# Weights stand and tokens move in 26 chunks of a decoder block on one Trainium2 core

## Chip, core and metric

The kernel runs on one NeuronCore of one Trainium2 chip. The metric is device time in microseconds for one execution. The profile shows one execution of the same program with every instruction of TensorE (PE, with its weight loads as PEld), VectorE (DVE), ScalarE (ACT), GpSimd (POOL) and the DMA queue of SyncE (SP).

## What is computed

One decoder layer on 256 tokens of width 2048, in float32: a SwiGLU feed-forward block, a token mixer (sparse attention beside multi-scale retention), and a second feed-forward block, each behind a modulated RMS norm. Cut to what the change touches:

```
h = modulate(x, ...)                              # 256 x 2048
x = x + 0.5*gt1 * (silu(h @ w_gate) * (h @ w_up)) @ w_down      # d_ff = 5632, once before and once after the mixer
u = modulate(x, ...)
q, kv, gate_logits, q_r, k_r, v_r, g_r, ga, gb = split(u @ w_in)
k_cmp, v_cmp = compress(kv[:, 0]), compress(kv[:, 1])           # 15 blocks of 32 tokens, stride 16, per group
    # compress: gelu((block + pos) @ cmp_w1 + b1) @ cmp_w2      # cmp_w1: 32*128 x 128
retention: scores = (q_r @ k_r.T) * decay ...
gates = sigmoid(gate_logits)
```

## The kernel before

**Parts.** A float32 operand is split in two parts that TensorE takes at full rate: `hi`, the operand rounded to fp32r by ScalarE, and `lo`, the remainder, by VectorE (`split`). A product is hi·hi + hi·lo + lo·hi. Activations have parts `ahi` and `alo` (tiles of 128 x 4 x 256, the model dimension on partitions), weights `whi` and `wlo`.

**Units and chunks.** All weights pass through one stream. A unit is 512 KB of it: one raw tile of 128 x 1024 (`raw`, six buffers), split to `whi` and `wlo` (four buffers each, lines 136 and 137). `run` issues loads as raw tiles come free and splits up to four items ahead of the unit that TensorE works on. A `chunk` computes 256 tokens x 512 outputs with the contraction over 16 tiles of 128: eight units, each 2 contraction tiles x 512 columns. In `unit`, tokens stand (128 x 128 of `ahi` or `alo` is the loaded operand) and weights move, 512 columns at a time: three matmuls for each half of the tokens and each contraction tile (lines 239 to 241), 96 in a chunk. The moving operand is read by turns: element j, then element j + 256, which lies 1 KB away (`by_turns`); `halves` undoes that when the result is read.

**What follows a chunk.** The result has tokens on partitions. Where it is next a contraction operand it is turned by eight TensorE transposes of 128 x 128 (`to_banks`, line 480): the gate·up product of every feed-forward chunk (`transposed`), the retention queries and keys (`retention.tr`), and the two compressed projections (`compress.tr`). Such later steps are put on a list, and one step is taken after each unit (`push`, `soon`).

**Around it.** `compress` multiplies 32 slices of the first layer in plain float32, 60 columns moving (line 923); its weights `cmp_w1` are loaded ahead, into free activation tiles (line 858). `gate_logits` takes 48 matmuls of 256 columns (lines 969 to 971). The first feed-forward block overlaps its first 6 chunk pairs with the modulation vectors (`early`, lines 688 to 690); loads for modulation (`w_ada`) are spread over the stream all along.

Of the kernel before, what the change touches and what calls it, by code (L numbers as in the profile page):

```python
# [18 lines left out]
P = 128  # L19
# [49 lines left out]
def block_kernel(ctx: ExitStack, tc: tile.TileContext, I, konst, decay, out):  # L69
# [9 lines left out]

    def act_hi(dt=F32R):  # L80
        return ap_.tile([P, 4, S], dt, tag="ahi", name="ahi")

    def act_lo(dt=F32R):
        return ap_.tile([P, 4, S], dt, tag="alo", name="alo")
# [550 lines left out]
    def ffn(l, his, los, last, first=None, head=None):  # L635
# [24 lines left out]

        def transposed(c, g):
# [61 lines left out]
        def both(c):  # L723
            g = [] if first and 2 * c < EARLY else chunk(act, src(wg, c), KT, NCH, gate_done(c), head=None if c else head)
# [127 lines left out]
    w1 = [[], []]  # L852
    for i in range(2):
        def ld(i=i):
            for b in range(4):
                w = act_hi(F32) if i == 0 else act_lo(F32)
                w = w.rearrange("p a s -> p (a s)").rearrange("p (j e) -> p j e", e=DH)
                nc.sync.dma_start(w, I["cmp_w1"][0, i, b * 8 * P:(b + 1) * 8 * P, :].rearrange("(j p) e -> p j e", p=P))
                w1[i].append(w)
        if i == 0:  # L860
            items.insert(len(items) - 60, ("do", lambda: clear()))
        at = len(items) - 10 - 8 * i
        items.insert(at, ("do", ld))
# [9 lines left out]
    def seg_chunk(c0, width, s, g, n, done):  # L873
# [4 lines left out]
        return chunk(u, src, KT, s * n, done)  # L878
# [17 lines left out]

    def compress(i):
        def done(ps):
            z = evac(ps)
            box = {}  # L900

            def tr():
                zT = t4([P, 4, S])
                banks = to_banks(lambda t, k: z[:, t, k * P:(k + 1) * P])
                for b in range(2):
                    nc.vector.tensor_copy(zT[:, 2 * b:2 * b + 2], banks[b])
                zp = []
                for h in range(2):
                    zz = t4([P, GROUPS, NCMP, 16])
                    src = bass.AP(tensor=zT.tensor, offset=zT.offset + 16 * h,  # L910
                                  ap=[list(zT.ap[0]), [S, GROUPS], [16, NCMP], [1, 16]])
                    pb = pos[:, i, 16 * h:16 * h + 16][:, None, None, :].to_broadcast([P, GROUPS, NCMP, 16])
                    nc.vector.tensor_tensor(zz, src, pb, op=ALU.add)
                    zp.append(zz)
                box["zp"] = zp

            def first_layer(b):
                def f():
                    if b == 0:
                        box["ps"] = mx()  # L920
                    for jj in range(8):
                        j = 8 * b + jj
                        nc.tensor.matmul(box["ps"][:, :60], w1[i][b][:, jj, :],  # L923
                                         box["zp"][j // 16][:, :, :, j % 16], start=j == 0, stop=j == 31)
                    if b == 3:
                        g = small(60, "g60")
                        nc.scalar.activation(g, box["ps"][:, :60], AF.Gelu_apprx_tanh, bias=b1[:, i:i + 1])
                        box["g"] = g
                return f

            def second_layer():
                g = box["g"]
                ps2 = mx()
                if i == 1:
                    for k in range(GROUPS):
                        nc.tensor.matmul(ps2[0:NCMP, k * DH:(k + 1) * DH], g[:, k * NCMP:(k + 1) * NCMP],
                                         w2[:, 1, :], start=True, stop=True)
                    v = ps2[0:NCMP, :].rearrange("p (g d) -> p g d", g=GROUPS)
                    for r in (0, 64):
                        nc.scalar.activation(vc[r:r + NCMP], v, AF.Copy)  # L940
                    nc.vector.tensor_tensor(vc[32:32 + NCMP], v, vc[0:NCMP].bitcast(F32), op=ALU.subtract)
                    return
                nc.tensor.matmul(ps2[0:60, :DH], g, w2[:, 0, :], start=True, stop=True)
                kn = t2([P, DH])
                junk = t2([P, DH])
                sc = small(1, "s1")
                nc.vector.tensor_copy(kn[0:60], ps2[0:60, :DH])
                nc.vector.scalar_tensor_tensor(junk[0:60], kn[0:60], 1.0, kn[0:60], op0=ALU.mult, op1=ALU.mult,
                                               accum_out=sc[0:60])
                nc.gpsimd.tensor_scalar(sc[0:60], sc[0:60], 1.0 / DH, EPS, op0=ALU.mult, op1=ALU.add)  # L950
# [9 lines left out]
            if i == 0:  # L960
                push(None, to_kcT)
# [415 lines left out]
```

## Time and profile before

| | us |
|---|---|
| median of three runs (2462.95 to 2465.0) | 2462.95 |
| the profiled execution | 2464.18 |
| its span, first to last instruction | 2462.4 |
| PE busy | 2425.2 |
| DVE busy | 1738.0 |
| ACT busy | 1219.8 |

PE is busy for 98% of the span and carries 88% of the chain that ended last. In the last feed-forward block (from 1800 us) the DMA engines move about 200 GB/s at 0.6 of their time, and DVE is busy for about half.

### The profile page before, as it was taken

How to read it: one execution, taken by the hardware profiler on the slowest of the kernel's cores; microseconds unless marked ns; L12 is line 12 of the kernel's file. 1: busy time of each engine (PE TensorE's matmuls, PEld its weight loads, DVE VectorE, ACT ScalarE, POOL GpSimd, SP SyncE). 2: the span in 40 equal slices, each digit the busy share in tenths (PEclk: the TensorE clock that was granted, in tenths of full speed). 3: DMA queues.
4: the chain of work that ended last, by engine and by line, in shares of the span. 5: the costliest groups of instructions: out<-in, count | busy, mean ns of one | idle time of the engine just before them, and what ended most of it. 6: DMA issues, size and time to landing. Idle time of an engine off the chain costs nothing.

```text
span 2462.4 us, 31664 instructions
## 1 busy us (share of the span) xinstructions
PE 2425.2 (98%) x11616; PEld 2116.0 (86%) x11616; DVE 1738.0 (71%) x2044; ACT 1219.8 (50%) x1584; POOL 139.8 (6%) x134
## 2 busy tenths in 40 slices
PE   6999999999999999999999999999999999999999
PEld 4888888888888888888888888888888888888887
DVE  7778878989656478886667777777788554555555
ACT  4788644444445455564444444444644444444443
POOL 1000001010010111200000000000000010001001
PEclk9999999999999999999999999999999999999999
DMA  9999888899776555667887777886599666666664
GB/s 354 337 323 344 286 318 310 294 314 341 273 231 193 148 150 171 193 215 268 281 269 257 250 256 256 274 269 235 180 342 325 203 205 198 197 202 202 202 199 152
DMA packets 348264, 616.65 MB, mean 250 GB/s; under 512 B 22096, under 2 KB 79926, under 8 KB 347852
## 3 DMA queue, kind: packets, MB, share of 16 engines
q1 hardware_dynamic: 347852, 614.51, 74.5%
q8 instruction: 91, 1.49, 0.2%
q14 instruction: 65, 0.53, 0.1%
q0 software_dynamic: 256, 0.12, 0.0%
HBM read 612.45 MB, written 2.10 MB: 250 GB/s over the span
## 4 chain that ended last, share of the span: by engine, by line
PE 88%; DVE 6%; DMA 3%; issue 2%; ACT 1%; POOL 0%; SPq 0%; DVEq 0%; ACTq 0%
PE accb L240 24%; PE accb L241 24%; PE accb L239 24%; PE accb L690 3%; PE accb L688 3%; PE accb L689 3%; DVE wlo L137 2%; DVE aacc L372 2%; DMA raw<-in_w_ffn_down_dram 2%; PE mx L480 1%; DMA raw<-in_w_ada_dram 1%; PE mx L923 1%; PE mx L1160 1%; ACT whi L136 1%; PE mx L1108 0%
## 5 line engine op out<-in xcount | busy, mean ns | idle before, releaser
L137 DVE TENSOR_TENSOR wlo<-raw,whi 128x1024 fp32r<-128x1024 f32 x852 | 1048.6, 1240 | 581.9 <-ACT whi L136 576.2
L136 ACT ACTIVATE whi<-raw 128x1024 fp32r<-128x1024 f32 x852 | 893.3, 1056 | 892.8 <-PE accb L241 690.8
L239 PE MATMUL accb<-whi,ahi 128*128 128x512 f32 x3072 | 1175.3, 383 | 1.3 <-ACT ahi L537 0.9
L240 PE MATMUL accb<-wlo,ahi 128*128 128x512 f32 x3072 | 1166.1, 380 | 3.4 <-DVE wlo L137 2.5
L241 PE MATMUL accb<-whi,alo 128*128 128x512 f32 x3072 | 1165.2, 379 | 1.2 <-DVE alo L605 1.2
L240 PEld LDWEIGHTS accb<-wlo,ahi 128*128 128x128 f32 x3072 | 580.8, 189 | 88.9 <-DVE wlo L137 5.6
L241 PEld LDWEIGHTS accb<-whi,alo 128*128 128x128 f32 x3072 | 580.6, 189 | 85.7 <-DVE alo L556 1.7
L239 PEld LDWEIGHTS accb<-whi,ahi 128*128 128x128 f32 x3072 | 580.8, 189 | 82.4 <-ACT ahi L537 2.0
L372 DVE SCALAR_TENSOR_TENSOR aacc<-raw,cond,aacc 128x1024 f32<-128x1024 f32 x270 | 352.0, 1304 | 1.7 <-DMA raw<-in_w_ada_dram 0.7
L626 POOL TENSOR_TENSOR x<-x,t 128x512 f32<-128x512 f32 x50 | 80.9, 1641 | 1553.0 <-DVE t L621 1553.0
L688 PE MATMUL accb<-whi,ahi 128*128 128x512 f32 x384 | 146.6, 382 | 0.0
L690 PE MATMUL accb<-whi,alo 128*128 128x512 f32 x384 | 145.8, 380 | 0.4 <-DVE alo L802 0.4
L689 PE MATMUL accb<-wlo,ahi 128*128 128x512 f32 x384 | 146.0, 380 | 0.0
L690 PEld LDWEIGHTS accb<-whi,alo 128*128 128x128 f32 x384 | 72.7, 189 | 11.1 <-DVE alo L802 0.8
L689 PEld LDWEIGHTS accb<-wlo,ahi 128*128 128x128 f32 x384 | 72.7, 189 | 10.6 <-DVE wlo L137 0.5
L688 PEld LDWEIGHTS accb<-whi,ahi 128*128 128x128 f32 x384 | 72.9, 190 | 10.1
L605 DVE TENSOR_TENSOR alo<-mx,ahi 128x512 fp32r<-128x512 f32 x52 | 33.5, 686 | 29.4 <-ACT ahi L604 29.3
L604 ACT ACTIVATE ahi<-mx 128x512 fp32r<-128x512 f32 x52 | 28.3, 597 | 46.9 <-PE mx L480 46.9
L621 DVE TENSOR_TENSOR t<-accb,gt 128x512 f32<-128x512 f32 x56 | 36.2, 684 | 7.8 <-PE accb L241 7.8
L647 ACT ACTIVATE t<-accb 128x512 f32<-128x512 f32 x44 | 25.7, 596 | 28.6 <-PE accb L241 20.3
L1123 ACT ACTIVATE t<-t,m 128x256 f32<-128x256 f32 (+1 forms) x64 | 28.2, 443 | 18.5 <-DVE m L1114 18.5
L883 ACT ACTIVATE t<-accb 128x512 f32<-128x512 f32 x44 | 25.8, 596 | 22.8 <-PE accb L241 22.7
(196 smaller groups left out, 1049.9 us busy)
## 6 DMA issues: line engine op xcount, KB each, us to landing
raw<-in_w_ada_dram SPq DMA_DIRECT2D x288, 512.0 KB, 5.7
raw<-in_w_ffn_gate_dram SPq DMA_DIRECT2D x176, 512.0 KB, 5.1
raw<-in_w_ffn_up_dram SPq DMA_DIRECT2D x176, 512.0 KB, 4.7
raw<-in_w_ffn_down_dram SPq DMA_DIRECT2D x176, 512.0 KB, 4.2
raw<-in_w_in_dram SPq DMA_DIRECT2D x176, 512.0 KB, 4.5
raw<-in_w_in_dram SPq DMA_DIRECT2D x128, 256.0 KB, 3.9
raw<-in_w_proj_nsa_dram SPq DMA_DIRECT2D x32, 512.0 KB, 5.8
raw<-in_w_proj_ret_dram SPq DMA_DIRECT2D x32, 512.0 KB, 5.6
```

Source lines behind the costliest of these rows:

```text
L136: nc.scalar.activation(hi_ap, raw_ap, AF.Copy)
L137: nc.vector.tensor_tensor(lo_ap, raw_ap, hi_ap.bitcast(F32), op=ALU.subtract)
L239: nc.tensor.matmul(ps[t], xh, wh, start=kt == 0, stop=False)
L240: nc.tensor.matmul(ps[t], xh, wl, start=False, stop=False)
L241: nc.tensor.matmul(ps[t], xl, wh, start=False, stop=kt == K - 1)
L372: nc.vector.scalar_tensor_tensor(box[0], raw, k, box[0], op0=ALU.mult, op1=ALU.add)
L605: nc.vector.tensor_tensor(lo[:, 2 * b:2 * b + 2], ps, h.bitcast(F32), op=ALU.subtract)
L621: nc.vector.tensor_tensor(in_two(y), halves(ps[t]), in_two(gt[:, n * NCH:(n + 1) * NCH]), op=ALU.mult)
L626: engine.tensor_tensor(xs, xs, y, op=ALU.add)
L688: nc.tensor.matmul(ps[t], xh, wh, start=kt + a == 0, stop=False, **kw)
L689: nc.tensor.matmul(ps[t], xh, wl, start=False, stop=False, **kw)
L690: nc.tensor.matmul(ps[t], xl, wh, start=False, stop=kt + a == k0 + nk - 1, **kw)
```

## The change

`turned_chunk` is new. It computes the same 256 tokens x 512 outputs as two sub-chunks of 256 outputs; a unit is now 4 contraction tiles x 256 columns. The weights stand, 128 x 128 at a time, and the tokens move: one matmul of `whi` against both token parts (512 columns, into the two halves of a bank) and one of `wlo` against the hi part (256 columns, added to the first half). `parts_by_turns` reads the tokens: element j, then element j + 128, which lies 512 bytes away. The result has outputs on partitions, so it is not transposed; `added` adds the two halves of the bank with a `tensor_reduce` on VectorE and puts the tokens in order. For that the two parts of an activation lie in one tile (`act_pair`).

It is used for the gate and up chunks 1 to 10 of the second feed-forward block (chunk 0 stays), retention's queries and keys (4 chunks) and the two compressed projections: 26 chunks of 512 outputs. Beside it:

- `cmp_w1` comes through the weight stream in eight loads and is split; a first-layer step multiplies parts of the blocks (120 columns stand) with 256 moving columns, and `fold` adds the parts afterwards in one small matmul. 
- The gate logits take 16 matmuls of 512 columns, both weight parts standing (96 columns).
- The mixer now begins with the keys and values of attention group 0, which take the `head` of the norm; the two compressed projections follow, then the gate logits and the queries of group 0.
- Retention's scores stand two units earlier on the list, since no transposes lie between.

```diff
+    def parts_by_turns(his, los, kt):
+        h, l = his[kt // 4][:, kt % 4], los[kt // 4][:, kt % 4]
+        return bass.AP(tensor=h.tensor, offset=h.offset,
+                       ap=[list(h.ap[0]), [l.offset - h.offset, 2], [1, P], [P, 2]])
+
+    def turned_chunk(his, los, src, K, done):
+        ps = []
+        def step(c, kt):
+            def f(hi, lo):
+                if kt == 0:
+                    ps[:] = [mx([P, 2, S]) for _ in range(2)]
+                for b in range(2):
+                    for a in range(4):
+                        k, bs = kt + a, slice(b * P, (b + 1) * P)
+                        both = parts_by_turns(his, los, k)
+                        nc.tensor.matmul(ps[b], hi[:, a, bs], both, start=k == 0, stop=False, skip_group_check=True)
+                        nc.tensor.matmul(ps[b][:, 0], lo[:, a, bs], both[:, 0], start=False, stop=k == K - 1,
+                                         skip_group_check=True)
+                if kt + 4 == K:
+                    done(c, ps)
+            return f
+        return [("w", src(kt, 4, c), 4, 256, step(c, kt)) for c in range(2) for kt in range(0, K, 4)]
+
+    def added(o, ps):
+        for b in range(2):
+            nc.vector.tensor_reduce(o[:, b].rearrange("p (t j) -> p j t", t=2),
+                                    ps[b].rearrange("p h (j t) -> p j t h", t=2), axis=AX.X, op=ALU.add)
...
+        def gate_turned(c):
+            def f(i, ps):
+                if i == 0:
+                    sg[c] = t4((P, 4, S))
+                g = sg[c][:, 2 * i:2 * i + 2]
+                added(g, ps)
+                nc.scalar.activation(g, g, AF.Silu)
+            return f
+        def up_turned(c):
+            def f(i, ps):
+                y = t2([P, 2, S])
+                added(y, ps)
+                g = sg[c][:, 2 * i:2 * i + 2]
+                nc.vector.tensor_tensor(g, y, g, op=ALU.mult)
+                if i == 1:
+                    push(*[None] * GAPS[0], in_parts_of(c, sg.pop(c)))
+            return f
...
-                        nc.tensor.matmul(box["ps"][:, :60], w1[i][b][:, jj, :],
-                                         box["zp"][j // 16][:, :, :, j % 16], start=j == 0, stop=j == 31)
...
+                    nc.tensor.matmul(box["ps"][0:120], box["Z", j // 16][:, j % 16].rearrange("p a c -> p (a c)"),
+                                     W[:, :, jj].rearrange("p a e -> p e a"), start=j == 0, stop=j == 31)
...
+            nc.tensor.matmul(ps[0:96], gl[kt // 8][:, kt % 8].rearrange("p a c -> p (a c)"), parts_by_turns(u_hi, u_lo, kt),
+                             start=kt == 0, stop=kt == KT - 1)
...
+    kv, q = attention(0)
+    mix += kv + z_chunk(0, done0) + after_units(z_chunk(1, done1), quarters0, 4)
+    mix += [("a", rows(win, 0, KT, O_GL, 48), KT, 48, gate_raw), ("do", gate_logits)]
+    mix += after_units(q, quarters1, 4)
...
-            push(None, tr, None, scores(0), scores(1))
+        def qk_done(c, ps):
+            if c == 0:
+                box["qkT"] = t4([P, 4, S])
+            added(box["qkT"][:, 2 * c:2 * c + 2], ps)
+            if c == 1:
+                dec = t2([P, 2, S])
+                nc.sync.dma_start(dec, decay[:, 2 * qd:2 * qd + 2, :])
+                box["dec"] = dec
+                push(None, scores(0), scores(1))
```

Three places of the program, as the instructions stand on an engine. On TensorE in the last feed-forward block before, `accb` is a chunk's bank, `t4` the gate·up product, `kc` the identity; the transposes stand two units into the next chunk:

```order
L239 MATMUL accb_15936<-whi_15903,ahi_14776 128x512
L240 MATMUL accb_15936<-wlo_15904,ahi_14776 128x512
L241 MATMUL accb_15936<-whi_15903,alo_14777 128x512
L480 MATMUL mx_15969<-kc_75,t4_15754 128x128 x4
L480 MATMUL mx_15974<-kc_75,t4_15754 128x128 x4
L239 MATMUL accb_15935<-whi_15923,ahi_14862 128x512
L240 MATMUL accb_15935<-wlo_15924,ahi_14862 128x512
```

And on TensorE now, at the seam of two sub-chunks of that block (`mx` is a sub-chunk's bank, `act` a tile with both token parts):

```order
L318 MATMUL mx_15737<-act_15057,whi_15762 128x512
L319 MATMUL mx_15737<-act_15057,wlo_15763 128x256
L318 MATMUL mx_15852<-act_14867,whi_15787 128x512
L319 MATMUL mx_15852<-act_14867,wlo_15788 128x256
L318 MATMUL mx_15852<-act_14867,whi_15787 128x512
```

Triples of 512 columns became pairs of 512 and 256, and no transpose stands between.

On VectorE in a retention chunk before, from the copies of the transposed queries and keys (line 1204) to the scores (1222, 1223, which read the decay table `t_10608`):

```order
L1204 COPY t_10636<-mx 128x512 x2
L137 TENSOR_TENSOR wlo<-raw,whi 128x1024
L372 SCALAR_TENSOR_TENSOR aacc<-raw,cond,aacc 128x1024
L137 TENSOR_TENSOR wlo<-raw,whi 128x1024
L1222 TENSOR_TENSOR t_10691<-mx,t_10608 128x256
L1223 TENSOR_TENSOR t_10691<-mx,t_10608 128x128
```

And now, from the sums of the second sub-chunk (line 329; the decay table is `t_10678`):

```order
L147 TENSOR_TENSOR wlo<-raw,whi 128x1024 x2
L329 TENSOR_REDUCE t_10572<-mx 128x128x2 x2
L416 SCALAR_TENSOR_TENSOR aacc<-raw,cond,aacc 128x1024
L1345 TENSOR_TENSOR t_10700<-mx,t_10678 128x256
L1346 TENSOR_TENSOR t_10700<-mx,t_10678 128x128
L147 TENSOR_TENSOR wlo<-raw,whi 128x1024 x2
```

The scores moved up, next to the end of the chunk that makes the queries and keys; the decay load is still issued at that end.

On VectorE at the first compressed projection before (copies of the turned bank, then the blocks with their positions):

```order
L137 TENSOR_TENSOR wlo<-raw,whi 128x1024 x2
L906 COPY t_6526<-mx 128x512 x2
L913 TENSOR_TENSOR t_6539<-t_6526,cols 128x960
L913 TENSOR_TENSOR t_6541<-t_6526,cols 128x960
L137 TENSOR_TENSOR wlo<-raw,whi 128x1024 x5
```

And now (lines 986 and 991 make the blocks and their lo part, `act<-raw,act` is the lo part of a quarter of `cmp_w1`):

```order
L329 TENSOR_REDUCE t_6606<-mx 128x128x2 x2
L986 TENSOR_TENSOR t_6701<-t_6606,cols 128x60x16
L991 TENSOR_TENSOR act<-t_6701,act 128x16x60
L147 TENSOR_TENSOR wlo<-raw,whi 128x1024
L147 TENSOR_TENSOR act<-raw,act 128x1024
L986 TENSOR_TENSOR t_6735<-t_6606,cols 128x60x16
L991 TENSOR_TENSOR act<-t_6735,act 128x16x60
L147 TENSOR_TENSOR wlo<-raw,whi 128x1024
L147 TENSOR_TENSOR act<-raw,act 128x1024
```

The queue has six more operations here between the end of a projection and the split of the units that TensorE takes next.

## Rows read from the trace of the kernel before

**Rows 1.** Page: busy time by engine; the chain that ended last
```profile
span 2462.4 us, 31664 instructions
...
PE 2425.2 (98%) x11616; PEld 2116.0 (86%) x11616; DVE 1738.0 (71%) x2044; ACT 1219.8 (50%) x1584; POOL 139.8 (6%) x134
...
PE 88%; DVE 6%; DMA 3%; issue 2%; ACT 1%; POOL 0%; SPq 0%; DVEq 0%; ACTq 0%
```

**Rows 2.** Windows: stretch and length, busy (instructions) per engine, clock, DMA share, GB/s
```profile
60.00:2400.00 2340.00, 2331.16 (x11211) 2039.09 (x11210) 1662.68 (x1966) 1171.73 (x1518) 121.64 (x114) 1.00 0.75 250
```

**Rows 3.** Timeline of PE, attention: start, length, operation; passes of 512, scores of 128
```profile
892.71 0.38 PE L239 MATMUL accb<-whi,ahi 128*128 128x512 f32 x1
...
896.38 0.38 PE L241 MATMUL accb<-whi,alo 128*128 128x512 f32 x1
896.60 1.95 PE L1108 MATMUL mx<-t,t 128*128 128x128 f32 x16
...
898.60 0.38 PE L240 MATMUL accb<-wlo,ahi 128*128 128x512 f32 x1
```

**Rows 4.** Timeline of PE, last feed-forward block: a product's eight transposes
```profile
1937.25 1.04 PE L480 MATMUL mx<-kc,t 128*128 128x128 f32 x8
...
1938.35 0.38 PE L240 MATMUL accb<-wlo,ahi 128*128 128x512 f32 x1
```

**Rows 5.** Timeline of PE, compress: one of eight first-layer steps
```profile
786.40 1.92 PE L923 MATMUL mx<-t,ahi 128*128 128x60 f32 x16
...
788.41 0.38 PE L240 MATMUL accb<-wlo,ahi 128*128 128x512 f32 x1
```

**Rows 6.** Timeline of PE, gate logits: the first and the last of 48
```profile
809.65 0.28 PE L969 MATMUL mx<-ahi,whi 128*48 128x256 f32 x1
...
815.14 0.28 PE L971 MATMUL mx<-ahi,wlo 128*48 128x256 f32 x1
```

**Rows 7.** Groups by form, PE and PEld: count, busy and mean ns, idle before
```profile
L480 PE MATMUL mx<-kc,t 128*128 128x128 f32 x256 | 33.4, 273 | 0.6 <-ACT t L883 0.6
...
L923 PEld LDWEIGHTS mx<-t,ahi 128*128 128x128 f32 x64 | 7.8, 192 | 0.2
...
L969 PEld LDWEIGHTS mx<-ahi,whi 128*48 128x48 f32 x16 | 1.9, 122 | 0.0
```

**Rows 8.** Groups by form, DVE and ACT: splits, operations of 512, a reduction of 512
```profile
L137 DVE TENSOR_TENSOR wlo<-raw,whi 128x1024 fp32r<-128x1024 f32 x851 | 1047.7, 1240 | 577.0 <-ACT whi L136 571.3 <-DMA raw<-in_w_in_dram 1.4
L605 DVE TENSOR_TENSOR alo<-mx,ahi 128x512 fp32r<-128x512 f32 x52 | 33.5, 686 | 29.4 <-ACT ahi L604 29.3
L913 DVE TENSOR_TENSOR t<-t,cols 128x960 f32<-128x960 f32 x4 | 4.5, 1155 | 0.1
L1114 DVE TENSOR_REDUCE m<-t 128x4 f32<-128x512 f32 x8 | 5.5, 686 | 0.3
...
L136 ACT ACTIVATE whi<-raw 128x1024 fp32r<-128x1024 f32 x851 | 892.5, 1056 | 892.8 <-PE accb L241 690.8 <-DMA raw<-in_w_ffn_down_dram 81.4 <-DMA raw<-in_w_ffn_up_dram 49.0
L604 ACT ACTIVATE ahi<-mx 128x512 fp32r<-128x512 f32 x52 | 28.3, 597 | 46.9 <-PE mx L480 46.9
```

**Rows 9.** Waits of PE, whole span: who waited for whom, total, times, longest
```profile
PE accb L240 <- DVE wlo L137: 2.5, 4, 1.1
```

**Rows 10.** Windows: loads in runs of 512 bytes, of 1 KB, of 2 KB
```profile
846.00:866.00 20.00, 20.00 (x94) 17.25 (x93) 10.75 (x16) 9.57 (x11) 6.03 (x8) 1.00 0.68 189
...
1209.00:1228.00 19.00, 19.00 (x90) 16.64 (x89) 12.41 (x12) 8.27 (x8) 0.00 (x0) 1.00 0.93 289
...
1950.00:2050.00 100.00, 100.00 (x465) 87.57 (x464) 55.17 (x47) 41.52 (x41) 14.11 (x8) 1.00 0.63 205
```

**Rows 11.** Timeline of PE, SP and DVE, fourth retention chunk: transposes, decay load, scores
```profile
1453.41 1.04 PE L480 MATMUL mx<-kc,t 128*128 128x128 f32 x8
...
1454.82 0.34 SPq L1197 DMA_DIRECT2D t<-decay_dram  x1
...
1461.63 0.42 DVE L1222 TENSOR_TENSOR t<-mx,t 128x256 f32<-128x256 f32 x1 [1.65 <-DMA t<-decay_dram]
```

More of the change, by code (lines that the diff above doesn't have):

```diff
@@ L659, in up_done, with turned, in_parts_of, f @@
             return f
+        def turned(c):
+            return not first and c > 0
+        def gate_turned(c):
[15 more added lines that the diff above has]
+            return f
+        def in_parts_of(c, g):
+            def f():
+                shi[c] = act_hi()
+                slo[c] = act_lo()
+                split_banks([g[:, 0:2], g[:, 2:4]], shi[c], slo[c])
+            return f
         def transposed(c, g):
@@ L851, in block_kernel @@
     u_hi, u_lo = [], []
[L852 to L863, printed above, removed]
+    items.insert(len(items) - 60, ("do", lambda: clear()))
     at_once, head = norm(xa2, u_hi, u_lo, r2_)
@@ L877, in src @@
             return v[:, :, :, g * n:(g + 1) * n]
-        return chunk(u, src, KT, s * n, done)
+        return chunk(u, src, KT, s * n, done, head=head)
     def evac(ps, func=AF.Copy):
@@ L895, in clear, with fold, done, placed @@
         nc.scalar.activation(pc3, ones[:, None, :CMP].to_broadcast([P, 8, CMP]), AF.Copy, scale=0.0)
+    def fold(n):
+        o = t2([P, P])[0:2 * n, 0:n]
+        nc.vector.tensor_tensor(o, ident[0:2 * n, 0:n], ident[0:2 * n, n:2 * n], op=ALU.add)
+        return o
     def compress(i):
[L898 to L909, printed above, removed]
+        box = {}
+        def done(c, ps):
+            if c == 0:
+                box["zT"] = t4([P, GROUPS, S])
+            zT = box["zT"]
+            added(zT[:, 2 * c:2 * c + 2], ps)
+            def placed(h):
+                def f():
+                    zz = t4([P, 16, GROUPS, NCMP])
+                    pb = pos[:, i, 16 * h:16 * h + 16][:, None, None, :].to_broadcast([P, GROUPS, NCMP, 16])
@@ L931, in second_layer @@
[L931 to L950, printed above, removed]
-                nc.gpsimd.tensor_tensor(sc[0:60], sc[0:60], mhalf[0:60, 0:1], op=ALU.pow)
-                nc.vector.tensor_scalar(kn[0:60], kn[0:60], sc[0:60], None, op0=ALU.mult)
-                box["kn"] = kn
@@ L955, in to_kcT @@
[L955 to L964 removed]
+                    nc.vector.tensor_tensor(zz.rearrange("p j g c -> p g c j"), src, pb, op=ALU.add)
@@ new lines, in to_kcT, with quarter, after_units @@
+        def to_kcT():
+            ps3 = mx()
+            nc.tensor.transpose(ps3[:, :60], box["kn"][0:60, :], ident[0:60, 0:60])
+            nc.vector.tensor_scalar(kcT, ps3[:, :60], g_qk[:, 1:2], None, op0=ALU.mult)
+        def quarter(b):
+            src = I["cmp_w1"][0, i, b * 8 * P:(b + 1) * 8 * P, :].rearrange("(j p) e -> p j e", p=P)
+            return [("a", src, 8, DH, w_parts(b)), ("do", first_layer(b))]
+        return done, [quarter(b) for b in range(4)]
+    def after_units(main, parts, at):
+        o, w = [], 0
+        parts = list(parts)
+        for it in main:
+            o.append(it)
+            w += it[0] == "w"
+            if it[0] == "w" and w >= at and parts:
+                o += parts.pop(0)
+        return o
```

150 lines of the change are left out of this document (98 added, 52 removed).

## Prediction

> **What bounds the kernel now.** I read the page first, then the windows, then PE's timeline at each operation that the change removes or resembles. TensorE is busy for 98% of the span and makes 88% of the chain that ended last [rows 1]. Between 60 and 2400 us it is idle for 2340.0 - 2331.2 = 8.8 us in all [rows 2], and in the whole span it waits for a split weight only four times, 2.5 us together [rows 9]. The granted clock is 1.00 there, the 2.4 GHz level. So the time is the sum of TensorE's passes, and another engine counts only where it becomes late. What one pass costs is read from start to start, not from the lengths shown, which overlap: 17 passes of 512 columns lie between 892.71 and 896.38, so one takes 3.67 / 17 = 0.2159 us [rows 3].
>
> **Removed: sixteen sets of transposes.** From the first of eight transposes to the second pass behind them are 1938.35 - 1937.25 = 1.10 us; less one pass, eight cost 0.884 us [rows 4]. They go in ten feed-forward pairs, four retention chunks and two projections: 16 x 0.884 = **14.1 us**, all on TensorE's path (128 of the 256 transposes of that form [rows 7]).
>
> **First layer of compress.** A step of eight float32 matmuls (sixteen records, two passes each) takes 788.41 - 786.40 - 0.216 = 1.794 us, 0.1121 a pass [rows 5]; eight steps are 14.35 us. Now 64 passes of 256 columns stand there, priced below at 0.1115: 7.1 us. Gain **7.2 us**.
>
> **Gate logits.** 48 passes, (815.14 - 809.65) / 47 = 0.1168 each [rows 6]: 5.6 us. Now 16 of 512 columns, 3.45 us. Gain **2.2 us**. The folds bring two float32 matmuls for the projections and two in place of two transposes: eight passes of 0.11 less two, **+0.7 us**.
>
> **The 26 turned chunks.** For each contraction tile and 128 outputs a pair replaces 1.5 old passes (96 passes a chunk become 64 pairs); 26 x 64 = 1664 pairs. Columns are equal, 768 against 768. New is that a pass of 256 columns must cover a weight load of 128 columns. No row shows this pair. The nearest is attention's scores: passes of 128 float32 columns, each behind a load of 128 columns, 898.60 - 0.216 - 896.60 = 1.784 us for sixteen, 0.1115 each [rows 3]. With only 60 columns moving the pace is the same, 0.1121 [rows 5], so there the load sets it, and I take the load as the bound of the short pass: pair 0.2159 + 0.1115 = 0.3274, against 0.3239; 1664 x 0.00355 = **+5.9 us**. Lower end: half a long pass, 0.1080, since the columns are not fewer; no cost. Upper end: the gate logits' 0.1168 [rows 6], +14.7 us; their load is shorter (122 against 192 ns [rows 7]), so something other than the load sets it.
>
> The Trainium skill, TensorE: Matmul & The Clock Gate, section Back-to-back issue gap, gives N / 2.4 + 2.5 ns for a warm pass. For 512 columns that is 0.2158, as the rows show; for 256 it would be 0.1092, and the sum would come out some 4 us lower.
>
> **What hides the rest.** VectorE gets 104 sums of a bank (no row shows this read; a reduction of 512 elements takes 0.686 us, as other operations of 512 do [rows 8]) and loses copies. At a seam between sub-chunks the order is: two sums 1.37, Silu 0.60, then the next split, 1.06 on ACT and 1.24 on DVE [rows 8], 4.3 us in all. Three split units of 2.6 us stand ready, 7.9 us: covered. Loads now come in runs of 1 KB: 289 GB/s at a share of 0.93 [rows 10] would be 311 GB/s when full, and a unit of 512 KB in 2.6 us asks for 200. The last block moved 205 GB/s at 0.63 in runs of 2 KB [rows 10]: covered. Taking the loads of the first layer's weights into the stream adds SP issues but no wait that TensorE sees.
>
> Two places lose their cover. In retention the scores now stand one unit behind the chunk. In the fourth chunk the queries' and keys' chunk ended one unit before the transposes, at 1453.41 - 2.59 = 1450.8, and VectorE waited for the decay table until 1461.63 [rows 11], 10.8 us later. If the table lands then, VectorE waits longer than before with the splits queued behind it: scores 0.7 and a split 1.24 end at 12.7, while TensorE reaches the first unsplit unit after four units and two scores of 0.65 each, at 11.7: some 0.8 us lost. In the other three the issue is earlier. At the second projection VectorE has two sums, two pairs of block operations (1.155 each, by the row of 960 [rows 8]) with a ScalarE copy of about 1.0 between, two first-layer splits and two unit splits: about 11.7 us, when TensorE needs the unit at about 11.6. Estimate for both: **+1 us**, from 0 to 4.
>
> **Sum.** -14.1 - 7.2 - 2.2 + 0.7 + 5.9 + 1.0 = -15.9 us on the profiled 2464.18, which gives 2448.3; the median of the runs lies 1.2 lower, so 2462.95 - 15.9 = **2447.0 us**. Ends: with 0.1080 and no stalls -14.1 - 7.4 - 2.2 + 0.7 = -23.0, 2440; with 0.1168 and 4 us of stalls -14.1 - 6.9 - 2.2 + 0.7 + 14.7 + 4 = -3.8, 2459.
>
> **Rivals.**
> *The moving read is slower (ends slower).* The order of reading matters in this trace: 256 columns read in sequence take 0.1168 behind a short load [rows 6], while half a pass read by turns at a distance of 1 KB takes 0.1080 [rows 3]. The new distance is 512 bytes and no row has it. At the sequential pace the pair is 0.2336 + 0.1168 = 0.3504, +0.0265 x 1664 = 44 us; with the other terms (first layer -6.9, gate logits -1.9) about +23, **2486 us**. It decides from a pair of 0.337, a long pass only 4.5% slower. For it: nothing but the unknown distance; against: 1 KB costs nothing. 0.09.
> The skill's Advanced Engine Details and Errata, SBUF Cachelines, says that a read which changes its line with each access is slower; the trace disagrees, since the hopping read is the fast one.
> *VectorE late at the seams (no gain).* If a sum takes 2.5 us instead of 0.686, the 3.6 us of cover is gone; 0.3 us at each of 52 seams would eat 15.6, **2463 us**. Speaks for it: the sum reads two places of a bank by turns; against: every bank read of 512 so far takes 0.69. 0.06.
> *The short pass is bounded by its columns alone.* Were the load hidden, at the price of 0.109 the pairs cost 2 us instead of 6: **2443 us**. Against: the scores' rows. 0.10. The gap rule cited above is this case.
> *The short pass runs as the gate logits did*, 0.1168: -14.1 - 6.9 - 2.2 + 0.7 + 14.7 + 1 = -6.8, **2456 us**. 0.08.
> That the change does not do what it says I leave out: the transposes are gone from the queue.
>
> **How the numbers follow.** Forecast 0.67, the rivals as given. About 0.2%, 4.9 us, is what a measurement here can tell from no change. Faster: forecast, columns alone and gate pace, 0.85, less 0.03 for stalls beyond my bound at the slow price: 0.82. Same: late seams less a part that ends slower, and that 0.03: 0.08. Slower: slow read 0.09 and 0.01 of the seams: 0.10. The range 2440 to 2460 holds the first three cases, 0.82; the slow read lies outside.
>
> **What would show it.** On PE's timeline in the last block, long and short passes should alternate at 0.216 and 0.112, no transposes, and the block be shorter by 10 x 0.884 - 1280 x 0.0036, 4 us. Short starts of 0.117, or long ones of 0.225 and more, show the two read cases; waits of PE for `wlo` above 5 us in total show late splits. First-layer passes at 0.112 carry 7 us of the gain. I am wrong if the pairs run above 0.337, or if PE's idle between 60 and 2400 us grows from 9 to 20 us or more.

## The result: 12 us slower, and the profile after

Five runs of the changed kernel gave a median of 2475.5 us (2473.2 to 2480.6) beside 2463.3 us for the kernel before (2463.0 to 2465.0). The ratio is 1.0053, with a 95% interval of 1.0041 to 1.0065: slower by 12 us by the medians and 13 by the ratio. The forecast was 2447.0, with a range of 2440 to 2460 and a chance of 0.10 for slower.

The page of the changed kernel: its span, busy time by engine, and the chain that ended last.

```profile
span 2471.2 us, 33017 instructions
...
PE 2415.9 (98%) x12230; PEld 2125.4 (86%) x12230; DVE 1810.3 (73%) x2154; ACT 1225.4 (50%) x1586; POOL 143.9 (6%) x134
...
PE 84%; DVE 9%; DMA 3%; issue 2%; ACT 1%; POOL 0%; SPq 0%; DVEq 0%; ACTq 0%
```

Against [rows 1], TensorE has 9 us less to do and the span is 9 us longer (the profiled execution is the fastest of the five, 2473.2 us). VectorE's share of the chain rose from 6% to 9%: TensorE now waits for it. Where it waits is read from the windows (stretch and length, then busy time and instructions of PE, PEld, DVE, ACT and POOL, the granted clock, DMA share, GB/s). First the changed kernel: the whole middle, attention, retention, and the first turned chunks of the last block.

```profile
60.00:2400.00 2340.00, 2312.88 (x11777) 2040.41 (x11777) 1728.89 (x2071) 1174.98 (x1517) 125.77 (x114) 1.00 0.75 250
860.00:1120.00 260.00, 250.15 (x1287) 219.22 (x1286) 206.80 (x393) 143.44 (x288) 32.55 (x34) 0.99 0.56 175
1290.00:1490.00 200.00, 193.41 (x999) 170.58 (x998) 145.49 (x192) 84.54 (x95) 5.56 (x12) 1.00 0.76 247
1800.00:1900.00 100.00, 95.98 (x563) 86.26 (x562) 88.44 (x87) 42.06 (x46) 0.00 (x0) 1.00 0.96 322
```

The same three stretches of the kernel before:

```profile
860.00:1120.00 260.00, 259.65 (x1346) 228.97 (x1346) 214.35 (x415) 146.89 (x292) 34.14 (x36) 1.00 0.60 187
1290.00:1490.00 200.00, 199.53 (x954) 174.86 (x954) 147.22 (x205) 88.48 (x101) 5.56 (x12) 1.00 0.78 251
1800.00:1900.00 100.00, 100.00 (x477) 87.76 (x476) 85.13 (x78) 46.52 (x52) 0.00 (x0) 1.00 0.94 340
```

TensorE's idle time in the middle is 2340.0 - 2312.9 = 27.1 us, against 8.8 in [rows 2]. Three stretches hold 20.5 of the 27.1, and with that all of the growth of 18.3: attention 9.9 against 0.4, retention 6.6 against 0.5, the start of the last block 4.0 against 0. The five largest waits of TensorE between 760 and 1900 us name the releasers (total, times, longest):

```profile
PE mx L319 <- DVE wlo L147: 5.6, 8, 1.4
PE mx L1276 <- DVE t L1263: 5.1, 4, 2.2
PE mx L1342 <- DVE t L329: 4.6, 3, 3.3
PE mx L1258 <- DVE t L1249: 4.3, 1, 4.3
PE mx L318 <- ACT whi L146: 1.3, 2, 0.7
```

L1276 and L1258 are attention (the product with the values, and the transposes of the probabilities), L1342 is retention's scores, L318 and L319 are the two passes of a pair. The trace of before has none of these in attention, and in retention one wait of 0.5 us for a split weight, among those of [rows 9].

**The passes came out as worked out.** TensorE's timeline in the changed kernel (start, length, operation): fourteen pairs in the last block, a first-layer step of compress, the gate logits.

```profile
813.77 1.04 PE L1011 MATMUL mx<-act 128*120 128x256 f32 x8
814.64 0.38 PE L318 MATMUL mx<-act,whi 128*128 128x512 f32 x1
...
824.25 3.62 PE L1084 MATMUL mx<-act,t 128*96 128x512 f32 x16
827.71 0.38 PE L249 MATMUL accb<-whi,act 128*128 128x512 f32 x1
...
1904.73 0.38 PE L318 MATMUL mx<-act,whi 128*128 128x512 f32 x1
1904.95 0.27 PE L319 MATMUL mx<-act,wlo 128*128 128x256 f32 x1
...
1909.31 0.38 PE L318 MATMUL mx<-act,whi 128*128 128x512 f32 x1
```

Fourteen pairs take 1909.31 - 1904.73 = 4.58 us, 0.327 each. A first-layer step takes 0.87 us against 1.79 in [rows 5], the gate logits 3.46 us against 5.6. So the passes were as short as forecast, and the gain was given back in waits and, as the last section shows, in a lower clock behind some of them.

**What each wait is.** In attention, on VectorE, ScalarE and TensorE of the changed kernel:

```profile
963.69 1.08 ACT L949 ACTIVATE t<-accb 128x512 f32<-128x512 f32 x2 [1.31 <-PE mx L1224]
965.93 0.28 DVE L1109 SCALAR_TENSOR_TENSOR t<-t 128x128 f32<-128x128 f32 x1
966.08 1.04 PE L1258 MATMUL mx<-kc,t 128*128 128x128 f32 x8
...
968.33 0.29 DVE L1109 SCALAR_TENSOR_TENSOR t<-t 128x128 f32<-128x128 f32 x1
...
974.64 1.28 DVE L1263 TENSOR_TENSOR t<-mx,t 128x512 fp32r<-128x512 f32 x2
975.38 1.08 PE L1276 MATMUL mx<-t,t 128*128 128x512 f32 x2 [2.22 <-DVE t L1263]
```

L949 takes the next group's queries out of their bank, and L1109 squares them, eight times between 965.93 and 968.54 (each with a short read of its sum behind it). This work lies in VectorE's queue right where the probabilities are transposed (L1258, from 966.08) and ahead of the split that TensorE needs of them (L1263), so the split comes 8.6 us after the transposes began, and TensorE waits 2.2 us for it. At the same place before, the split came 6.1 us after them, and TensorE went through its six passes without a wait:

```profile
961.72 1.04 PE L1142 MATMUL mx<-kc,t 128*128 128x128 f32 x8
967.77 1.91 PE L1160 MATMUL mx<-t,t 128*128 128x512 f32 x6
967.86 1.28 DVE L1147 TENSOR_TENSOR t<-mx,t 128x512 fp32r<-128x512 f32 x2
```

The reason is the list of later steps. When the queries of group 0 end, it still holds six places in the changed kernel: the last four of the second projection (empty, `to_g`, empty, `second_layer`: the projection's activation and its second layer), an empty one and the gates' `tr`. Attention's list is put behind them. It has 17 steps for the 16 units of a group, so nothing makes up for that: counted so, every step of all four groups stands six units later against the ends of the chunks.

In retention the chain is shorter. TensorE waits at the scores in three of the four chunks; this is the longest. The scores stand one unit behind the chunk, and the sums of their own queries and keys (L329) stand behind two splits on VectorE, which waited for ScalarE:

```profile
1387.70 3.88 ACT L146 ACTIVATE whi<-raw 128x1024 fp32r<-128x1024 f32 x4
1388.78 2.36 DVE L147 TENSOR_TENSOR wlo<-raw,whi 128x1024 fp32r<-128x1024 f32 x2 [0.46 <-ACT whi L146]
1391.06 1.28 DVE L329 TENSOR_REDUCE t<-mx 128x256 f32<-128x512 f32 x2
1391.80 0.70 PE L1342 MATMUL mx<-t 128*128 128x256 f32 x2 [3.33 <-DVE t L329]
```

At the start of the last block ScalarE is the link:

```profile
1866.60 1.06 ACT L146 ACTIVATE whi<-raw 128x1024 fp32r<-128x1024 f32 x1 [3.35 <-DMA raw<-in_w_ffn_gate_dram]
1868.83 1.28 DVE L329 TENSOR_REDUCE t<-mx 128x256 f32<-128x512 f32 x2
1870.15 0.63 ACT L714 ACTIVATE t<-t 128x512 f32<-128x512 f32 x1 [2.49 <-DVE t L329]
...
1871.73 1.04 ACT L146 ACTIVATE whi<-raw 128x1024 fp32r<-128x1024 f32 x1
...
1873.74 1.22 DVE L147 TENSOR_TENSOR wlo<-raw,whi 128x1024 fp32r<-128x1024 f32 x1
1875.01 0.38 PE L319 MATMUL mx<-act,wlo 128*128 128x256 f32 x1 [1.38 <-DVE wlo L147]
```

ScalarE stands 2.5 us at Silu (L714) until VectorE has summed, with the split of the next weights queued behind it. Until about 1890 us the loads for modulation run beside the weights (DMA share 0.96 above between 1800 and 1900), and the split had itself waited 3.35 us for its load, so no split unit was in hand.

### The profile page after: what moved, and what is told of

It reads as the page before. It is cut to its first block, busy times and chain, and to the rows that moved or that the text cites. A ratio compares the mean times of both kernels' runs of the same rounds, so it can differ in the third digit from the quotient of the medians.

```text
span 2471.2 us, 33017 instructions
## 1 busy us (share of the span) xinstructions
PE 2415.9 (98%) x12230; PEld 2125.4 (86%) x12230; DVE 1810.3 (73%) x2154; ACT 1225.4 (50%) x1586; POOL 143.9 (6%) x134
## 4 chain that ended last, share of the span: by engine, by line
PE 84%; DVE 9%; DMA 3%; issue 2%; ACT 1%; POOL 0%; SPq 0%; DVEq 0%; ACTq 0%
PE accb L250 17%; PE accb L251 17%; PE accb L249 17%; PE mx L318 12%; PE mx L319 6%; PE accb L762 3%; PE accb L761 3%; PE accb L763 3%; DVE wlo L147 3%; DVE aacc L416 2%; DMA raw<-in_w_ffn_down_dram 1%; ACT whi L146 1%; PE mx L524 1%; PE mx L1224 1%; DMA raw<-in_w_ada_dram 1%
## 5 line engine op out<-in xcount | busy, mean ns | idle before, releaser
L249 PE MATMUL accb<-whi,act 128*128 128x512 f32 x2240 | 857.5, 383 | 1.3 <-ACT act L581 0.9
L250 PE MATMUL accb<-wlo,act 128*128 128x512 f32 x2240 | 851.2, 380 | 2.1 <-DVE wlo L147 1.1
L251 PE MATMUL accb<-whi,act 128*128 128x512 f32 x2240 | 850.7, 380 | 0.3 <-DVE act L649 0.3
L318 PE MATMUL mx<-act,whi 128*128 128x512 f32 x1664 | 549.1, 383 | 1.3 <-ACT whi L146 1.3
L250 PEld LDWEIGHTS accb<-wlo,act 128*128 128x128 f32 x2240 | 424.2, 189 | 64.9 <-DVE wlo L189 3.8
L251 PEld LDWEIGHTS accb<-whi,act 128*128 128x128 f32 x2240 | 423.8, 189 | 62.9 <-DVE act L600 1.7
L249 PEld LDWEIGHTS accb<-whi,act 128*128 128x128 f32 x2240 | 424.2, 189 | 60.7 <-ACT act L581 2.0
L319 PE MATMUL mx<-act,wlo 128*128 128x256 f32 x1664 | 454.6, 273 | 5.6 <-DVE wlo L147 5.6
L318 PEld LDWEIGHTS mx<-act,whi 128*128 128x128 f32 x1664 | 314.5, 189 | 45.1 <-ACT whi L146 1.8
L319 PEld LDWEIGHTS mx<-act,wlo 128*128 128x128 f32 x1664 | 319.4, 192 | 8.7 <-DVE wlo L147 8.1
L761 PE MATMUL accb<-whi,act 128*128 128x512 f32 x384 | 146.6, 382 | 0.0
L762 PE MATMUL accb<-wlo,act 128*128 128x512 f32 x384 | 146.2, 381 | 0.1
L763 PE MATMUL accb<-whi,act 128*128 128x512 f32 x384 | 145.8, 380 | 0.4 <-DVE act L879 0.4
L762 PEld LDWEIGHTS accb<-wlo,act 128*128 128x128 f32 x384 | 72.7, 189 | 11.3 <-DVE wlo L147 1.2
L763 PEld LDWEIGHTS accb<-whi,act 128*128 128x128 f32 x384 | 72.7, 189 | 11.0 <-DVE act L879 0.8
L761 PEld LDWEIGHTS accb<-whi,act 128*128 128x128 f32 x384 | 72.9, 190 | 10.1
L329 DVE TENSOR_REDUCE t<-mx 128x256 f32<-128x512 f32 x104 | 66.8, 686 | 0.0
```

Of the source, the lines that this page charges most:

```text
L249: nc.tensor.matmul(ps[t], xh, wh, start=kt == 0, stop=False)
L250: nc.tensor.matmul(ps[t], xh, wl, start=False, stop=False)
L251: nc.tensor.matmul(ps[t], xl, wh, start=False, stop=kt == K - 1)
L318: nc.tensor.matmul(ps[b], hi[:, a, bs], both, start=k == 0, stop=False, skip_group_check=True)
L319: nc.tensor.matmul(ps[b][:, 0], lo[:, a, bs], both[:, 0], start=False, stop=k == K - 1, skip_group_check=True)
L761: nc.tensor.matmul(ps[t], xh, wh, start=kt + a == 0, stop=False, **kw)
```

## The experiments

The theory after this reading: three covers were lost, each by the place of a step in a queue. The general rival: VectorE's added work (72 us more busy) costs the time, wherever it stands. Each ratio below is to the kernel before, run beside it.

### Attention's list, first try

```diff
+    follow = {}
...
-                    soon(None, to_g, None, second_layer, *([None, to_kcT] if i == 0 else []))
+                    if i == 0:
+                        soon(None, to_g, None, second_layer, None, to_kcT)
...
+        follow[i] = (to_g, second_layer)
...
+        if g == 0:
+            steps[1], steps[3] = follow[1]
```

> The changed kernel, with one edit: the two last steps of the second compressed projection take two of the three empty places in attention group 0's own list of steps, so that all attention steps stand where they stood before the change, four units earlier than in the changed kernel. Theory A (attention's steps came four units late, so that the norm of the next queries, eight VectorE sums of 0.33 us, falls between a step's transposes and its split): TensorE's waits at L1276 and L1258 (9.4 us by the page of waits, 12.9 by start to start between 900 and 1110 us) go, and with them the two half-clock stretches of 3.4 us that follow two of them; 2475.5 - 13 to 16 = 2459 to 2463. Rival B (VectorE is simply loaded more, or group 0's keys and values hold buffers longer since they stand ahead of the projections): the waits stay or move to the splits, 2473 to 2477.

Measured: 2463.4 us, ratio 0.9998 (0.9989 to 1.0007), 0.4 us above theory A's range and almost 10 below rival B's. The waits at both attention lines are gone and so are the 13 us. VectorE's work is the same, and the keys and values of group 0 still stand ahead of the projections, so rival B and the general rival fall for this place. The "four units" of the expectation was a miscount: six places stood ahead, and this edit takes four of them away.

### The kernel before, with attention's list later

```diff
-            push(*steps)
+            push(*([None] * 4 if g == 0 else []), *steps)
```

> The kernel before, with one edit: four empty steps ahead of attention group 0's list, so that all attention steps come four units later, and nothing else changes. Theory A: the place of the steps alone is the cause, and the same waits of TensorE for VectorE appear here (about 13 us, and 1.7 us for each half-clock stretch): 2473 to 2479. Rival B: no wait of more than 2 us appears, 2462 to 2466.

Measured: 2469.0 us, ratio 1.0020 (1.0010 to 1.0029). Neither value: about 5 us, not 12. The waits at the product with the values appear (3.8 us in three), the long one at the transposes does not. With the count put right the dose was too small, so it was given again with six:

```diff
-            push(*steps)
+            push(*([None] * 6 if g == 0 else []), *steps)
```

> The kernel before, with six empty steps ahead of attention group 0's list. Counted in the traces, the list starts 0.6 units behind its chunk before, 6.6 in the changed kernel (not four, as written for the first two runs), 2.6 in the first and 4.6 in the second experiment, which cost 5.4 us. Theory A (the place alone costs): six cost what the changed kernel pays there, 2473 to 2477 (before 2463.5 plus 10 to 13). Rival B (the place costs 5 us, the rest comes from VectorE's added work): 2467 to 2471.

Measured: 2476.0 us, ratio 1.0050 (1.0036 to 1.0063), theory A. Six empty places, and nothing else, make the old kernel as slow as the changed one. TensorE's waits in its attention stretch are almost those of the changed kernel, under the line numbers of before:

```profile
PE mx L1160 <- DVE t L1147: 4.9, 4, 2.2
PE mx L1142 <- DVE t L1133: 4.3, 1, 4.3
```

In the changed kernel two places more than none cost nothing that can be measured (the first try, and the next run); in the kernel before, four cost 5 us and six cost 12. The cost is not in proportion: it appears when the norm of the queries reaches the transposes and their split.

### Attention's list exactly where it was

Beside the edit of the first try:

```diff
-        push(None, tr)
-    gl = {}
+        box["tr"] = tr
+    gl, box = {}, {}
+    follow["gates"] = lambda: box["tr"]()
...
+        if g == 0:
+            steps[1], steps[3] = follow[1]
+            steps[2] = follow["gates"]
```

> The changed kernel with attention's list where it stood before the change: the two last steps of the second projection and the last step of the gates take the three empty places of group 0's list, so nothing stands ahead of it. Theory A: another 0 to 3 us less than with the list two units late (2463.4), 2460 to 2463, with 900 to 1110 us free of added stalls. Rival B: as the first experiment or slower, 2463 to 2466.

Measured: 2463.3 us, ratio 0.9998 (0.9988 to 1.0007). As with two places: rival B's value. The last two were free.

### Retention's scores two units later

```diff
-                push(None, scores(0), scores(1))
+                push(None, None, None, scores(0), scores(1))
```

> The changed kernel, with one edit: retention's two steps of scores stand two units later, as many units behind the chunk as before the change. Theory (the scores came so early that TensorE waits for the sums of their own queries and keys, which stand behind splits on VectorE): TensorE's wait at the scores for the sums (4.6 us, 5.4 by start to start) goes, 2475.5 - 5 = 2470 to 2472, and the wait of VectorE for the decay table (16.2 us) falls too. Rival (VectorE is behind with everything at this place): the same 5 us appear at the splits, 2474 to 2477.

Measured in the changed kernel: 2471.6 us, ratio 1.0028 (1.0017 to 1.0040), 3.9 us less by the medians and some 6 by the ratios, the value of the theory. TensorE's wait at the scores is gone, about 1 us of it came out again at the next splits (1.9 us there between 1290 and 1490 us before the move, 3.0 after), and VectorE's wait for the decay table fell. The two rows of VectorE's waits, of the changed kernel and then of this one:

```profile
DVE t L1345 <- DMA t<-decay_dram: 16.2, 4, 4.6
```

```profile
DVE t L1345 <- DMA t<-decay_dram: 1.3, 1, 1.3
```

TensorE's waits for splits did not shrink with it, so what TensorE paid for here was the wait for the sums, not VectorE's wait for the table.

With attention's list in place:

> Attention's list where it stood before the change, and retention's scores two units later; the last block as changed. The stalls between 1300 and 1500 us were 10.5 us with the list alone and 4.7 with all three moves. Theory: 2463.3 - 5 to 6.5 = 2457 to 2458.5. Rival (worth the 3.9 us that it gave in the changed kernel): 2459 to 2460.5.

Measured: 2455.9 us, ratio 0.9976 (0.9966 to 0.9987): by the ratios 5.4 us less than the list alone, the gain that the theory gives (the kernel before measured 2462.0 us beside this run and 2463.8 beside that one). TensorE's idle time between 1290 and 1490 us is 4.0 us less than with the list alone. The profile with the list alone also has 3.4 us at half the granted clock (the 1.2 GHz level; see the last section) right behind the wait of 3.3 us, which cost 1.7, and this one has none.

### Silu one unit later

```diff
                 added(g, ps)
-                nc.scalar.activation(g, g, AF.Silu)
+                push(None, lambda: nc.scalar.activation(g, g, AF.Silu))
```

> The changed kernel, with one edit: in the last feed-forward block the Silu of a turned sub-chunk is issued one unit later, so that ScalarE splits the next unit before it waits for VectorE's sums. Theory (ScalarE stands at Silu until VectorE has summed, with the split of the next weights queued behind it; this meets units that arrive just in time, since the loads for modulation run beside the weights until about 1890 us): the five stalls between 1838 and 1887 us (5.5 us by start to start) fall by 4 or more, 2470 to 2472. Rival (the transfers are the limit in that stretch, 0.95 of their time busy, and TensorE only waits for them): the stalls stay within 1 us of 5.5, 2474 to 2477.

Measured in the changed kernel: 2473.5 us, ratio 1.0040 (1.0025 to 1.0055): neither value, in the right direction, but within the spread. The profiles show a reason why this move and that of the scores gave so little by the medians in the changed kernel. TensorE's idle time fell by 3.0 us here and by 3.1 there, but its time at half clock between 60 and 2400 us, 6.8 us in the changed kernel, was 17.1 here and 13.7 there, and half of that time is lost. ScalarE's wait at Silu fell from 56.9 us in 20 times to this:

```profile
ACT t L714 <- DVE t L329: 3.9, 3, 2.3
```

> Attention's list where it stood before the change (alone 2463.3 us), and in the last feed-forward block the Silu of a turned sub-chunk one unit later; retention as changed. The stalls between 1800 and 1900 us were 6.1 us with the list alone and 3.2 with all three moves, in passes from start to start. Theory (the Silu's place is worth what the stalls show): 2463.3 - 3 to 4.5 = 2458.5 to 2460.5. Rival (worth the 2.0 us that it gave in the changed kernel, or less): 2461 to 2463.5.

Measured with attention's list in place: 2458.6 us, ratio 0.9983 (0.9973 to 0.9992): the theory's value, by the ratios 3.7 us less than the list alone, just more than their spread (about 3.3). The transfers are not the limit by themselves: between 1800 and 1900 us ScalarE waits for its loads as long as before (34.2 us, 31.5 in the changed kernel), but TensorE's idle time there is 0.7 us, against 3.1 with the list alone.

### All three moves

> All three moves at once: attention's list where it was, retention's scores two units later, the Silu of a turned sub-chunk one unit later. If the three lost covers are all that failed and their gains add: 2475.5 - 13 - 4 - 4 = 2453 to 2457, faster than before by 0.3%. If the added VectorE work comes out at another place each time: 2460 to 2464.

Measured: 2453.5 us, ratio 0.9959 (0.9946 to 0.9973): the value of the theory, 10 us faster than before and 23 us faster than the change as made. 13.6 for the list, 5.4 for the scores and 3.7 for Silu add to 22.7, so within the spread the three gains are separate and make up what this kernel gained on the change as made. Of the 19.7 us between the two profiled executions, 14.5 are idle time of TensorE and 3.4 the half clock that followed waits, of which this kernel has none between 60 and 2400 us. The windows of this kernel, same stretches as above:

```profile
60.00:2400.00 2340.00, 2327.39 (x11875) 2055.50 (x11874) 1740.42 (x2083) 1182.07 (x1524) 122.84 (x114) 1.00 0.76 251
860.00:1120.00 260.00, 259.60 (x1348) 228.69 (x1347) 213.93 (x401) 148.47 (x295) 30.34 (x34) 1.00 0.59 185
1290.00:1490.00 200.00, 196.98 (x1004) 173.99 (x1003) 150.60 (x205) 87.41 (x97) 3.86 (x9) 1.00 0.79 257
1800.00:1900.00 100.00, 98.19 (x591) 88.98 (x590) 93.01 (x94) 48.30 (x54) 0.00 (x0) 1.00 0.95 322
```

TensorE idles 12.6 us in the middle, 3.8 more than before; attention is back at 0.4, retention keeps 3.0 and the last block 1.8. VectorE is as busy as in the changed kernel (1740 us against 1729), so the general rival falls: the place of its work cost the time, not the amount.

### Which part of the change brings the gain

The same kernel, with retention's queries and keys computed as before the change and the scores as they were then:

```diff
...
-        return (turned_chunk(u_hi, u_lo, qk, KT, qk_done)
+        return (seg_chunk(O_QR, 1024, 2, qd, 256, qk_done)
```

> As the run before it, but retention's queries and keys are computed as before the change (tokens stand, eight transposes, scores where they were). By the passes alone this is slower by 4 x 0.884 - 256 x 0.0036 = 2.6 us than the run before it. If TensorE still waits some 4 us for VectorE in the four turned chunks of retention, it is faster by 1 to 3 us.

Measured: 2454.9 us, ratio 0.9962 (0.9948 to 0.9976). Neither value: the turned chunks of retention win 0.7 us by the ratios, less than can be told from nothing. And with the feed-forward chunks as before, too:

```diff
         def turned(c):
-            return not first and c > 0
+            return False
```

> Attention's list where it stood before the change, and of the turned chunks only the two compressed projections are left (with the first layer and the gate logits as changed); the feed-forward chunks and retention are computed as before the change. By starts in the trace of the kernel with all three moves a pair takes 0.2184 + 0.1097 = 0.3281 us against 1.5 x 0.2158 = 0.3238 of before, so 128 pairs and sixteen transposes of a feed-forward chunk pair cost what they save to within 0.3 us: -8.8 + 1280 x 0.0043 = -3.3 us for ten, and its stalls at the start of the block take 3 of them back. Theory (the feed-forward chunks bring nothing, retention 1 to 2 us, nearly all of the gain is that of the projections, the first layer and the gate logits): 2454 to 2457. Rival (the feed-forward chunks bring their 8.8 us of transposes): 2460 to 2464.

Measured: 2455.5 us, ratio 0.9968 (0.9955 to 0.9980). Some 8 of the 10 us come from the two projections, the first layer and the gate logits. Twenty turned chunks of the feed-forward block are worth 1.5 us by the ratios, which cannot be told from nothing either.

### The order in which the tokens are read

```diff
+            return bass.AP(tensor=h.tensor, offset=h.offset, ap=[list(h.ap[0]), [l.offset - h.offset, 2], [1, S]])
...
-                        both = parts_by_turns(his, los, k)
+                        both = in_row(k)
...
-                                    ps[b].rearrange("p h (j t) -> p j t h", t=2), axis=AX.X, op=ALU.add)
+            nc.vector.tensor_reduce(o[:, b], ps[b].rearrange("p h j -> p j h"), axis=AX.X, op=ALU.add)
```

> The kernel with all three moves, but the turned chunks read the tokens in a row (256 elements of the hi part, then 256 of the lo part) and not by turns at a distance of 512 bytes; the sums on VectorE then read the bank's halves in order. If reading in a row costs what the gate logits' rows of the kernel before suggest (0.1168 for 256 columns against 0.1080 by turns), a pair takes 0.345 to 0.350 in place of 0.328, 1664 pairs 28 to 37 us more: 2480 to 2491. If the order of reading costs nothing and another cause stood behind the gate logits' pace (their short load): 2452 to 2456.

Measured: 2484.1 us, ratio 1.0082 (1.0067 to 1.0097), 30 us slower than reading by turns. TensorE's timeline of this kernel, fifteen pairs apart:

```profile
1929.66 0.39 PE L322 MATMUL mx<-act,whi 128*128 128x512 f32 x1
1929.89 0.28 PE L323 MATMUL mx<-act,wlo 128*128 128x256 f32 x1
...
1934.87 0.39 PE L322 MATMUL mx<-act,whi 128*128 128x512 f32 x1
```

5.21 / 15 = 0.347 a pair, 0.020 more than by turns; averaged over all pairs without a stall it is 0.350 against 0.3275. For 1664 pairs that is 33 to 38 us. The slower pace hides some waits: TensorE's idle time between 60 and 2400 us is 7.7 us here, 4.9 less than in the kernel with all three moves. A sum on VectorE takes 0.686 us in both orders.

## Why the prediction was wrong, step by step

- **Bound, pass lengths, removals: right.** A first-layer step measures 0.87 us (forecast 0.89), the gate logits 3.46 (3.45), a pair 0.327 (0.3274); averaged over all pairs without a stall it is 0.3275. So the passes are worth -14.1 - 7.4 - 2.1 + 0.7 + 5.3 to 7 = -16 to -17.6, and the sum had -16.9 before its last term. One reading was short: TensorE waited for split weights eight times in the kernel before, not four (another four under line 179, 0.9 us), which changes nothing in the sum.
- **How the pair is made up: partly right.** The forecast had the weight load as the bound of the short pass, 0.1115. On average the short pass takes 0.109 and the long one 0.218, so the split between the two was not as forecast, while the total was. The Trainium skill, TensorE: Matmul & The Clock Gate, section Back-to-back issue gap, would give 0.1092 for the short pass, an estimate by the page's formula for an isolated matmul; the mean start distance of 0.109 agrees. The sum still did not come out lower, since the long pass took 0.218 and not 0.2158.
- **The moving read: the price right, the condition not met.** Reading in a row costs 0.347 a pair, near the 0.3504 of that rival; a distance of 512 bytes costs nothing against 1 KB (the gate logits read so and take 3.46 / 16 = 0.216 a pass of 512; why the long pass of a pair takes 0.218 stays open). The Trainium skill, Advanced Engine Details and Errata, section SBUF Cachelines, has a penalty for each access that goes to another line; for TensorE's moving operand here the trace shows the opposite, since reading by turns takes 0.327 and reading in a row 0.347.
- **The step that failed: "What hides the rest", +1.0 us from 0 to 4.** The three moves won back 22.7 us, almost all of it put at nothing there. Three statements of that step were wrong.
  - *"Taking the loads of the first layer's weights into the stream adds SP issues but no wait that TensorE sees."* No wait for these loads is among the five above, but the steps that follow them were not counted on the list. Six places ahead of attention's list cost 12 to 13.6 us, the largest term of all, and it was not in the sum or in any rival.
  - *"Three split units of 2.6 us stand ready, 7.9 us: covered."* The transfers were judged by the middle of the last block (205 GB/s at a share of 0.63 in [rows 10]) for all of it, as the section on the time before does from 1800 us on. Between 1800 and 1900 us they were at 340 GB/s and a share of 0.94 before the change as well, and the lines shown from 1866.60 have no split unit in hand. The chain named (sums, Silu, split) was the right one: 3.7 us.
  - *Retention's scores one unit behind the chunk.* The place was right, the mechanism wrong. The forecast followed the decay table, which VectorE does wait for (16.2 us in all). TensorE waited earlier, for the sums themselves, which stood behind two splits at the longest wait: 5.4 us with the clock that followed, where 0.8 was set.
- **The second projection: right place, priced too low.** TensorE waits there once, 0.9 us at 811.3, against a 0.1 worked out. The terms that the forecast lists add to 11.95 us and not 11.7, and it counts one copy of ScalarE where VectorE waits for two (1.1 us each). The queues shown for this place differ by four operations, not six. The forecast priced the block operations by the old row, 1.155 [rows 8]; the changed ones write with a stride and take 1.97:

```profile
L986 DVE TENSOR_TENSOR t<-t,cols 128x960 f32<-128x960 f32 x4 | 7.9, 1970 | 0.1
```

- **The sums on VectorE: right**, 0.686 us each, 104 of them. The rival "VectorE late at the seams" had the right engine and the wrong reason: the sum is not slow; where it stands in VectorE's queue, and what stands behind the wait for it, cost the time.
- **Its own test worked.** It would be wrong, it said, if the idle time of TensorE grew from 9 to 20 us or more; it grew to 27. Its sign of late splits, more than 5 us of waits for `wlo`, came too: 5.6 between 760 and 1900 us.

What stays open: with all three moves the kernel gains 10 us, not the 16 of the forecast. Of the 6 us between, 2.8 are idle time of TensorE beyond the 1.0 that the sum had, and up to 1 the pairs; some 2 us were not traced. The last block was to be 4 us shorter and hardly is: from its first pass at 1752.2 us to the end of the span 699.3 us, against 700.0 from 1762.4 before; 1.8 us of the difference are idle time left at its start.

## What to carry to other kernels

Where later steps wait on a list and one is taken after each unit, an inserted step moves all behind it: count the places ahead of each list before and after, and see which engine's work of the next chunk then falls between a step's producer and its consumer. Read the cover of a wait from the stretch in which it is needed, not from the block's average; at a share of 0.94 to 0.96 nothing was in hand here. A helper operation on ScalarE that waits for VectorE holds back the splits queued behind it; issuing it one unit later won 3.7 us here.

## What the runs showed of the hardware

**The order of reading sets the pace of a pass.** The same 512 columns in the same two tiles take 0.22 us read by turns and 0.23 in a row, and 256 columns 0.11 and 0.12. The gate logits of [rows 6] had raised the suspicion; a kernel that differs in the order alone (and in the sums that undo it) is 30 us slower.

**The granted clock falls after some waits.** The windows of the changed kernel around the 2.2 us wait in attention (5 us, 4 us, 4 us):

```profile
972.00:977.00 5.00, 2.67 (x15) 1.84 (x14) 4.60 (x10) 4.88 (x18) 0.63 (x1) 1.00 0.22 60
977.00:981.00 4.00, 4.00 (x14) 3.30 (x12) 3.79 (x10) 2.12 (x4) 0.00 (x0) 0.57 0.60 190
981.00:985.00 4.00, 4.00 (x24) 3.57 (x23) 4.00 (x6) 1.08 (x2) 0.00 (x0) 1.00 0.62 204
```

And TensorE's timeline within it: six passes from 977.71 to 980.27, 0.427 each in place of 0.216, the 1.2 GHz level.

```profile
977.71 0.63 PE L250 MATMUL accb<-wlo,act 128*128 128x512 f32 x1
...
980.27 0.48 PE L250 MATMUL accb<-wlo,act 128*128 128x512 f32 x1
```

TensorE was busy for 2.67 of the 5 us ahead of it. The lost clock is worth 4.00 x (1 - 0.57) = 1.7 us on top of the wait. Between 60 and 2400 us the changed kernel's profile has two such stretches (behind the wait of 2.2 us and at the end of the one of 4.3 us in attention) and none at the 3.3 us wait in retention. With attention's list where it was, the same wait was followed by one: the two passes shown above with 0.70 us at 1391.80 then took 1.22.

```profile
1379.26 1.22 PE L1351 MATMUL mx<-t 128*128 128x256 f32 x2 [3.33 <-DVE t L329]
```

So a wait of this size does not always bring one, and the time of a kernel with such waits moves by more than the waits themselves.
